# Four moved steps in a one-core hybrid encoder step: DRAM copies of T4, the load of T1, a convolution gate, a reciprocal

## The chip, the cores and the metric

The kernel runs on one core of a Trainium2 chip. The metric is the device time of one execution in microseconds (us). Three executions of the kernel before took 1503.79, 1504.84 and 1506.19 us; the median, 1504.84 us, is the time to compare with. A further execution was taken by the hardware profiler.

The engines have the names of the profile: PE is TensorE (matrix products), PEld its weight load, DVE is VectorE, ACT is ScalarE, POOL is GpSimd, and SP is the queue from which most DMAs are issued. Each engine runs its own instructions in order and waits on semaphores for the others.

## What is computed

One layer of an encoder, for 1024 prompt frames and 32 sample frames (1056 columns in all), in float32:

```python
h = rmsnorm(x, g_mix)
proj = h @ w_in                                   # q, k, v, cb, cc, cx, ga, gc
y_attn = attend(q, k, v).reshape(b, t, SB_WIDTH) @ w_attn_out
conv_out, new_buf = causal_conv(cc * cx, conv_buf, conv_w)
y_conv = (cb * conv_out) @ w_conv_out
merged = jax.nn.sigmoid(ga) * y_attn + jax.nn.sigmoid(gc) * y_conv
x = x + merged @ w_o
f = jnp.square(jax.nn.relu(rmsnorm(x, g_ffn) @ w_up)) @ w_down
x = x + f
x = x + jax.nn.sigmoid(rmsnorm(x, g_ple) @ w_ple_gate) * (p @ w_ple)
```

The model width is 1024, the inner width of the MLP 4096. The outputs are the normed x, the keys, the values and the last convolution inputs.

## The kernel before, in words

**Products.** Activations lie with features on the 128 partitions and frames along the free dimension. Each float32 operand is split into a high and a low part (a copy to fp32r on ScalarE, a subtraction on VectorE), and a product is three matmuls: high by high, high by low, low by high. The large products, `x @ w_in` and the `w_up` half of the MLP, are done by a scheme of Strassen's kind (Winograd's form): of the quarters of weights and activations, sums (S1 to S4, T1 to T4) are formed, and seven products replace eight. Two sets of 256 output features are run together as a pair (`seven_pair`, L560); within a pair part of the products is split once more, by the operands called inner (`prepare_inner`, L256) and last (`prepare_last`, L298, `last_operands`, L336).

**Steps.** `seven_pair` is a generator that yields after each product of 12 matmuls, 25 times in a pair. `run` (L809) takes one step of it and then one step of every generator on the list `side`, in the order of the list. All the other work hangs on this list: loads of the next weights, their splits, what follows a set's outputs (scaling by the inverse norm, gates, stores). `after(n, ...)` (L772) puts a generator off by n steps. Where an instruction stands in the program is therefore a matter of yields. The order on PE, DVE, ACT and POOL is kept as written throughout, that on SP in the stage of the `w_up` pairs 2 to 15 (L2631).

**The buffers.** Most tiles of one row of 1056 columns come from one pool of 37 buffers (`blk`, L93). A new tile takes a buffer that was released before, and its first writer waits until the last reader of the old tile is done, a DMA among them.

**Around T4 and T1 (pairs of the `w_up` stage).** In pair 2 and 3 the operand T4 is used whole. From pair 4 on (`both`, L2003) its product too is split, and needs operands that are built once, during pair 2, 3, by `last_operands("u", ...)` (L2636): it starts one step late, fetches raw T-sums from DRAM (`rlu`, L2636 in the profile), copies blocks of T4 to the DRAM tiles zduB11, zduB21 and zduB22 (L348, six DMAs of 264 KB on SP; there is no B12), and then, twice, forms sums on VectorE (L354, L357), a high part `dlu` on ScalarE (L362), a low part on VectorE (L366), and stores both to the DRAM tile zduT (L368). The first of the two rounds begins its sums at step 7 of the pair, the second at step 14; its stores are issued at step 17. In each later pair, `z_load` (L372) brings these blocks back into SBUF (ztB, ztT; L374): B11 after the first product, T1 after the third, the rest later. `outer("A11", "B11")` uses the first in step 8, `outer("S1", "T1")` the second in step 9 (L634, L645). The copies ACT L635, L647 and L653 free the PSUM tile that the next group needs. Of the previous set, `mid_sums` (L1943) forms three sums and a difference on VectorE and stores them from SP (mdT, L1948 to L1957), `up_hooks` stores the squared outputs (mdB, L1968). The weights of the next pair are loaded into four raw buffers (raw_u4r, raw_u4o, raw_u4e and so on; L115, L212, L207) and split or summed by `prepare` (L217).

**Around the convolution's gate.** `conv_gate` (L1166), for the four column blocks nb of cb, scales (L1079, in `scaled`), multiplies by the convolution's result (L1169), waits 8 steps for odd and 3 for even nb, makes the high part `cvh` (ACT, L1173) and issues its store from ScalarE's queue (L1174), and a step later makes the low part (DVE, L1176) and stores it from SP (L1177). Behind it come the keys of the next set, `keys_or_queries` (L1083), whose scaling is again L1079 and whose high parts are L1089 to L1093.

**Around the reciprocal.** `stats_x` (L956) squares the rows of x on ScalarE, takes the root (ACT, L967) and the reciprocal (DVE, L968) of the nine sums per partition, waits six steps, and spreads the result over the columns.

Of the kernel before, what the change touches and what calls it, by code (L numbers as in the profile page):

```python
# [9 lines left out]
F32 = mybir.dt.float32  # L10
# [65 lines left out]
def tile_step(  # L76
# [8 lines left out]
    nc = tc.nc  # L85
# [7 lines left out]
    def blk(name, dt=F32, shape=None):  # L93
        return bpool.tile(shape or [P, T], dt, tag="B", name=name)
# [56 lines left out]
    quarters = [slice(t * TQ, (t + 1) * TQ) for t in range(4)]  # L151
    oper = {k: [None] * 4 for k in ("B11", "B12", "B21", "B22", "T1", "T2", "T3", "T4")}
# [183 lines left out]
    def last_operands(nm, load):  # L336

        def fetch_raw(k):
            r = blk(f"rl{nm}{k}", F32, [P, 4, TQ])
            for i in range(2):  # L340
                load(r[:, 2 * i : 2 * i + 2, :], k + 2 * i)
            return r

        raw = fetch_raw(0)
        for b, j0, f in (("B11", 0, 0), ("B21", 2, 0), ("B22", 2, 1), ("B12", 0, 1)):
            if b in zd[nm]:
                for j in range(2):
                    nc.sync.dma_start(zd[nm][b][:, :, j, :], oper["T4"][j0 + j][:, :, quarters[f]].bitcast(F32))  # L348
        for k in range(2):
            for _ in range(5 - k):  # L350
                yield
            x = [raw[:, i, :] for i in range(4)]
            for o, a, b, op in ((3, 3, 1, sub), (1, 0, 1, sub)):
                dve(x[o], x[a], x[b], op=op)  # L354
            yield
            for o, a, b, op in ((0, 0, 3, add), (2, 2, 0, sub)):
                dve(x[o], x[a], x[b], op=op)  # L357
            yield
            d, done_ = blk(f"dl{nm}{k}", F32R, [P, 4, TQ]), raw
            if k == 0:  # L360
                raw = fetch_raw(1)
            nc.scalar.copy(d, done_)  # L362
            yield
            for h in range(2):
                c = slice(2 * h, 2 * h + 2)
                dve(done_[:, c, :].bitcast(F32R), done_[:, c, :], d[:, c, :].bitcast(F32), op=sub)  # L366
            for part, src in ((0, d.bitcast(F32)), (1, done_)):
                nc.sync.dma_start(zd[nm]["T"][:, :, part, k, :].rearrange("a p t -> p a t"), src)  # L368

    zt = {}  # L370

    def z_load(nm, b):  # L372
        zt[b] = t = blk(f"zt{b}", F32R, [P, 2, 2, TQ])
        nc.sync.dma_start(t.bitcast(F32), zd[nm]["T"]["T2 T1 T4 T3".split().index(b)] if b[0] == "T" else zd[nm][b])  # L374
# [185 lines left out]
    def seven_pair(s0, s1, key, m, last, after=({}, {}), both=None, more=None):  # L560
# [13 lines left out]
        def inner(a, b, on=None, pool_=few):  # L574
            return inner_product(f"{a}{key}", ws[key][a], b, on, pool_)

        def done(i, k):
            after[i].get(k, int)()
# [14 lines left out]
        def third(i, t):  # L593
            product(i, "S2", "T2", t, x[i][t])
            u2[i][t] = tile_of("u2", t)
            nc.scalar.copy(u2[i][t], x[i][t])  # L596

        def fourth(i, t):
            product(i, "S3", "T3", t, x[i][t])
            dve(m(i, 1)[:, q[t][2]], x[i][t], s5[i][t], op=sub)  # L600

        def fifth(i, t):
            product(i, "S4", "B22", t, z[i][t])
            dve(m(i, 0)[:, q[t][2]], u2[i][t], z[i][t], op=sub)
# [5 lines left out]
        def outer(a, b, on=None, pool_=few):  # L610
            return inner_product(f"l{a}{key}", ws[f"{key}l"][a], zt.pop(b), on, pool_)
# [4 lines left out]
        def seven_both():  # L616
            for f in (first, second):
                for t in range(2):
                    f(0, t)
                    yield  # L620
                    if f is first and t == 0:
                        z_load(both, "B11")
                    if f is second and t == 0:
                        z_load(both, "T1")
            third(0, 0)
            yield
            third(0, 1)
            yield
            fourth(0, 0)
            yield  # L630
            tmp = blk(f"tmp{key}", F32, [P, 4, TQ])
            p4, s4, u4 = (tmp[:, i, :] for i in range(3))
            v4 = wpool[0].tile([P, TQ], F32, tag="v4", name=f"v4{key}", bufs=1)
            xl = outer("A11", "B11", pool_=tps)  # L634
            nc.scalar.copy(p4, xl)  # L635
            fourth(0, 1)
            yield
            z_load(both, "T2")
            z_load(both, "B21")
            done(0, "22")  # L640
            xi = inner("A11", "B11")
            dve(p1[0], xi, p1[0], op=add)
            fifth(0, 0)
            yield
            zl = outer("S1", "T1")  # L645
            z_load(both, "B22")
            nc.scalar.copy(s4, zl)  # L647
            fifth(0, 1)
            done(0, "12")
            yield  # L650
            zi = inner("S1", "T1")
            i5 = tile_of("s5", 2)
            nc.scalar.copy(i5, zi)  # L653
            inner("S2", "T2", xi)
            dve(p1[1], xi, p1[1], op=add)
            yield
            outer("S2", "T2", xl)
            dve(v4, xl, s4, op=sub)
            c11 = inner("A12", "B21", pool_=many)
            dve(m(0, 0)[:, q[0][1]], c11, p1[0], op=add)  # L660
            yield
            c[1] = tile_of("p1", 2)
            inner("S3", "T3", xi)
            dve(c[1], xi, i5, op=sub)
            outer("A12", "B21", x[0][0])
            fold(0, 0, p4)
            yield
            z_load(both, "T3")
            second(1, 0)
            yield  # L670
            inner("S4", "B22", zi)
            dve(m(0, 0)[:, q[1][1]], p1[1], zi, op=sub)
            done(0, "11")
            first(1, 1)
            yield
            c[0] = tile_of("p1", 3)
            inner("A22", "T4", xi)
            nc.scalar.copy(c[0], xi)
            outer("S4", "B22", x[0][1])
            fold(0, 1, v4)  # L680
            yield
            z_load(both, "T4")
            done(0, "21")
            first(1, 0)
            done(1, "11")
            yield
            second(1, 1, few)
            yield
            outer("S3", "T3", xl)
            dve(v4, xl, s4, op=sub)  # L690
            nc.scalar.copy(u4, xl)
            third(1, 1)
            yield
            third(1, 0)
            yield
            fifth(1, 1)
            yield
            fourth(1, 0)
            yield
            fifth(1, 0)  # L700
            done(1, "12")
            done(1, "near")
            yield
            fourth(1, 1)
            outer("A22", "T4", x[1][0])
            fold(1, 1, v4)
            fold(1, 0, u4)
            done(1, "22")
            done(1, "21")
            yield  # L710
            for k in (s0, s1, key, f"{key}l"):
                ws.pop(k)
# [243 lines left out]
    def stats_x():  # L956

        nc.vector.memset(ssq, 1.0)
        for i in range(9):
            n = P if i < 8 else DEC  # L960
            r = rows[i % 3][:n, :]
            nc.scalar.activation(r, r, AF.Square, accum_out=ssq[:n, i : i + 1])
            if i < 6:
                load_rows(i + 3)
            for _ in range(3 if i in (2, 5) else 1):
                yield
        nc.scalar.activation(rst, ssq, AF.Sqrt, bias=eps_t, scale=1.0 / D)  # L967
        nc.vector.reciprocal(rst, rst)  # L968
        for _ in range(6):
            yield  # L970
        nc.scalar.preload_act_table_set("sigmoid_and_others")
        for q0 in (0, 3, 6):
            yield from spread(rst, rs, q0)
            yield
# [8 lines left out]
    def md(k, s_):  # L983
# [11 lines left out]
    zd = {  # L995
        nm: {k: dpool.tile([P, 2, 2, TQ], F32, name=f"zd{nm}{k}") for k in ("B11", "B21", "B22")}
        for nm in ("u",)
    }
# [167 lines left out]
    def conv_gate(nb, m):  # L1166
        scaled(m)
        yield
        dve(m, m, cst.pop(("y", nb)), op=ALU.mult)  # L1169
        for _ in range(8 if nb % 2 else 3):  # L1170
            yield
        h = blk(f"cvh{nb}", F32R)
        nc.scalar.copy(h, m)  # L1173
        nc.scalar.dma_start(cvd[nb, 0], h.bitcast(F32))  # L1174
        yield
        dve(m.bitcast(F32R), m, h.bitcast(F32), op=sub)  # L1176
        nc.sync.dma_start(cvd[nb, 1], m)  # L1177
        yield
# [561 lines left out]
    with tc.manual_schedule(engines=MM):  # L1740
        next(sample)
        for n in range(len(steps) + LAG + 1):
# [13 lines left out]
            for op in ORDER:  # L1756
# [9 lines left out]
                elif op == "G" and n > LAG and steps[n - LAG - 1][2] % 2 == 1:  # L1766
                    p, j, i_ = steps[n - LAG - 1]
# [248 lines left out]
    first = {}  # L2016
# [632 lines left out]
    with tc.manual_schedule(engines=MM):  # L2649
# [68 lines left out]
        for u in range(8, 23):  # L2718
            t = u // 8 - 1
# [84 lines left out]
```

## Time and profile before

| what | value |
|---|---|
| median of three executions | 1504.84 us |
| the profiled execution | 1508.1 us |
| its span, first to last instruction | 1506.2 us |
| mean granted TensorE clock | 0.999 |
| DVE, ACT, POOL busy | 79%, 53%, 25% of the span |
| moved by DMA, mean over the span | 201 GB/s |

The kernel runs through these stages: input products to about 427 us, attention with embedding and convolution products in between to 607 us, branch and output projections to about 747 us, the `w_up` products to about 1070 us, `w_down` to about 1394 us, and the per-layer embedding with the last norm.

How to read it: times of the profile are microseconds from the start of the span, and lines L... are those of the kernel before. A row of the timeline gives start, duration, engine, line and operation, output and inputs by the program's names, the shapes, and in brackets the idle time of the engine just before it and what ended it. That releaser is inferred from semaphores: of several that a wait needs it is the one that came last by the profile. SPq and ACTq are the DMA issues of those queues. Matmuls overlap their predecessors, so a busy TensorE shows rows that start every 0.12 us though each lasts 0.28.

### The profile page before, as it was taken

What the parts mean: (1) busy time and instruction counts of PE and PEld (TensorE: products, weight loads), DVE (VectorE), ACT (ScalarE), POOL (GpSimd) and SP (SyncE); (2) the same over time, 40 slices, a digit from 0 to 9 for tenths busy, and PEclk for the clock granted to TensorE, in tenths of its full rate; (3) what the DMA queues carried; (4) which work ended last, traced back from release to release, by engine and by line L of the source; (5) the groups of instructions that cost most, each with busy time, mean ns of one, the idle gap of its engine ahead of it and who ended that gap; (6) DMA issues with size and microseconds to landing.
All of it is one profiled execution on the core that took longest, in us unless ns stands there. A gap on an engine that the chain in (4) does not pass through costs nothing.

```text
span 1506.2 us, 29625 instructions
## 1 busy us (share of the span) xinstructions
PE 1489.3 (99%) x11520; PEld 1475.5 (98%) x11520; DVE 1187.2 (79%) x1716; ACT 802.8 (53%) x1595; POOL 378.3 (25%) x326
## 2 busy tenths in 40 slices
PE   9999999999999999999999999999999999999997
PEld 8999999999999999999999999999999999999997
DVE  6867689779578999876788777888688878879766
ACT  7654444444467767433475555565655433334655
POOL 0433334445121223003323334334000000000251
PEclk9999999999999999999999999999999999999999
DMA  6624425422688666745647677766979767855433
GB/s 242 209 79 171 157 71 190 155 81 100 216 273 262 188 168 153 264 143 187 231 156 258 238 243 258 250 229 233 374 288 284 241 192 237 293 185 167 141 130 121
DMA packets 127772, 303.37 MB, mean 201 GB/s; under 512 B 14960, under 2 KB 35568, under 8 KB 127632
## 3 DMA queue, kind: packets, MB, share of 16 engines
q1 hardware_dynamic: 122512, 286.97, 56.3%
q0 software_dynamic: 1728, 6.29, 2.4%
q10 hardware_dynamic: 3392, 8.23, 1.7%
q8 instruction: 90, 1.47, 0.4%
q14 instruction: 50, 0.41, 0.1%
HBM read 219.89 MB, written 89.93 MB: 206 GB/s over the span
## 4 chain that ended last, share of the span: by engine, by line
PE 89%; DVE 4%; ACT 3%; DMA 3%; issue 1%; ACTq 0%; SPq 0%; DVEq 0%
PE ps_dn L2232 6%; PE ps_dn L2233 6%; PE ps_dn L2231 6%; PE ps_A11i L453 4%; PE ps_A11i L454 4%; PE ps_A11i L455 4%; PE ps_A11u L453 3%; PE ps_A11u L454 3%; PE ps_A11u L455 3%; PE av L1495 3%; PE ps_wo L133 2%; PE ps_wo L135 2%; PE ps_wo L134 2%; PE ps_S1i L455 2%; PE ps_S1i L454 2%; PE pa L1476 2%
## 5 line engine op out<-in xcount | busy, mean ns | idle before, releaser
L2232 PE MATMUL ps_dn<-flP,whi_dn 128*128 128x264 f32 x768 | 218.3, 284 | 0.0
L2231 PE MATMUL ps_dn<-fhP,whi_dn 128*128 128x264 f32 x768 | 218.3, 284 | 0.0
L2233 PE MATMUL ps_dn<-fhP,wlo_dn 128*128 128x264 f32 x768 | 218.3, 284 | 0.0
L2231 PEld LDWEIGHTS ps_dn<-fhP,whi_dn 128*128 128x128 f32 x768 | 144.5, 188 | 0.0
L2233 PEld LDWEIGHTS ps_dn<-fhP,wlo_dn 128*128 128x128 f32 x768 | 144.5, 188 | 0.0
L2232 PEld LDWEIGHTS ps_dn<-flP,whi_dn 128*128 128x128 f32 x768 | 144.5, 188 | 0.0
L1440 DVE TENSOR_TENSOR_SCAN r<-r 128x128 f32<-128x128 f32 (+3 forms) x64 | 86.9, 1358 | 5.3 <-POOL r L1433 5.3
L2446 POOL TENSOR_TENSOR xx<-xx,pgs 128x400 f32<-128x400 f32 (+1 forms) x17 | 20.0, 1184 | 281.5 <-DVE pgs L2445 281.5
L453 PE MATMUL ps_A11i<-T,shS_i 128*128 128x264 f32 x288 | 82.4, 286 | 0.7 <-ACT u_i L596 0.7
L455 PE MATMUL ps_A11i<-T,slS_i 128*128 128x264 f32 x288 | 82.0, 285 | 0.4 <-DVE slS_i L251 0.4
L454 PE MATMUL ps_A11i<-T,shS_i 128*128 128x264 f32 x288 | 82.2, 285 | 0.0
L453 PE MATMUL ps_A11u<-T,shS_u 128*128 128x264 f32 x256 | 73.1, 286 | 1.8 <-ACT u_u L596 1.7
L454 PE MATMUL ps_A11u<-T,shS_u 128*128 128x264 f32 x256 | 72.9, 285 | 0.0
L455 PE MATMUL ps_A11u<-T,slS_u 128*128 128x264 f32 x256 | 72.7, 284 | 0.0
L2075 ACT CAST whi_dn<-raw_dn 128x1024 fp32r<-128x1024 f32 x31 | 32.6, 1052 | 69.8 <-PE ps_dn L2232 51.1
L1433 POOL TENSOR_SCALAR_AFFINE_SELECT r<-r 128x128 f32<-128x128 f32 x64 | 37.6, 588 | 127.8 <-ACT r L1426 127.8
L2097 DVE TENSOR_TENSOR flP<-mrP,fhP 128x1056 fp32r<-128x1056 f32 x48 | 60.1, 1251 | 2.7 <-ACT fhP L2092 2.6
L135 PE MATMUL ps_wo<-mh,wlo_wo 128*128 128x352 f32 x192 | 62.0, 323 | 0.0
L134 PE MATMUL ps_wo<-ml,whi_wo 128*128 128x352 f32 x192 | 61.9, 323 | 0.0
L133 PE MATMUL ps_wo<-mh,whi_wo 128*128 128x352 f32 x192 | 61.8, 323 | 0.0
L251 DVE TENSOR_TENSOR slS_i<-s_i,shS_i 128x512 fp32r<-128x512 f32 x54 | 48.3, 895 | 13.2 <-ACT shS_i L191 12.8
L1480 DVE TENSOR_TENSOR at<-pa,at 128x512 fp32r<-128x512 f32 (+2 forms) x96 | 50.3, 546 | 10.3 <-ACT at L1479 9.4
(2058 smaller groups left out, 5825.1 us busy)
## 6 DMA issues: line engine op xcount, KB each, us to landing
raw_dn<-in_w_down_dram SPq DMA_DIRECT2D x59, 512.0 KB, 5.4
mrP<-mdT SPq DMA_DIRECT2D x32, 528.0 KB, 5.9
mdB<-m SPq DMA_DIRECT2D x48, 264.0 KB, 2.5
ztT<-zduT SPq DMA_DIRECT2D x24, 528.0 KB, 5.4
mrP<-mdB SPq DMA_DIRECT2D x24, 528.0 KB, 6.2
ztB<-zduB SPq DMA_DIRECT2D x18, 528.0 KB, 4.9
s<-gd SPq DMA_DIRECT2D x16, 528.0 KB, 6.1
mdT<-ta SPq DMA_DIRECT2D x32, 264.0 KB, 2.3
```

What stands on the lines that cost most here:

```text
L133: nc.tensor.matmul(ps, wh, xh[k][:, cols], start=(k == order[0]), stop=False)
L134: nc.tensor.matmul(ps, wh, xl[k][:, cols], start=False, stop=False)
L135: nc.tensor.matmul(ps, wl, xh[k][:, cols], start=False, stop=(k == order[-1]))
L453: nc.tensor.matmul(p_, wh[:, k, :], h, start=new and n == 0, stop=False, **on)
L454: nc.tensor.matmul(p_, wh[:, k, :], l, start=False, stop=False, **on)
L455: nc.tensor.matmul(p_, wl[:, k, :], h, start=False, stop=z, **on)
L1440: nc.vector.tensor_tensor_scan(rev, rev, rev, 1.0, ALU.mult, ALU.bypass)
L1480: nc.vector.tensor_tensor(al, pt[:, :nb, :], ah.bitcast(F32), op=ALU.subtract)
L2097: dve(l, mraw.pop(v), opd[v].bitcast(F32), op=sub)
L2231: nc.tensor.matmul(ps, hi[:, j, :], oh, start=j == 0, stop=False)
L2232: nc.tensor.matmul(ps, hi[:, j, :], ol, start=False, stop=False)
L2233: nc.tensor.matmul(ps, lo[:, j, :], oh, start=False, stop=j == NP_ - 1)
```

## The change

The six copies of T4's blocks move from the start of `last_operands`, behind its first two loads, to its end, behind the second round's stores; there is a yield before each block, and the entry for B12, which had no effect, goes. In `seven_both` the load of T1 is issued after the second product of the pair instead of the third. `stats_x` yields once between the root and the reciprocal, and once less after it. `conv_gate` waits 7 steps instead of 8 for odd blocks.

```diff
@@ last_operands
         raw = fetch_raw(0)
-        for b, j0, f in (("B11", 0, 0), ("B21", 2, 0), ("B22", 2, 1), ("B12", 0, 1)):
-            if b in zd[nm]:
-                for j in range(2):
-                    nc.sync.dma_start(zd[nm][b][:, :, j, :], oper["T4"][j0 + j][:, :, quarters[f]].bitcast(F32))
         for k in range(2):
...
             for part, src in ((0, d.bitcast(F32)), (1, done_)):
                 nc.sync.dma_start(zd[nm]["T"][:, :, part, k, :].rearrange("a p t -> p a t"), src)
+        for b, j0, f in (("B11", 0, 0), ("B21", 2, 0), ("B22", 2, 1)):
+            yield
+            for j in range(2):
+                nc.sync.dma_start(zd[nm][b][:, :, j, :], oper["T4"][j0 + j][:, :, quarters[f]].bitcast(F32))
@@ seven_pair
                     f(0, t)
                     yield
-                    if f is first and t == 0:
-                        z_load(both, "B11")
-                    if f is second and t == 0:
-                        z_load(both, "T1")
+                    if f is first:
+                        z_load(both, "T1" if t else "B11")
@@ stats_x
         nc.scalar.activation(rst, ssq, AF.Sqrt, bias=eps_t, scale=1.0 / D)
+        yield
         nc.vector.reciprocal(rst, rst)
-        for _ in range(6):
+        for _ in range(5):
             yield
@@ conv_gate
-        for _ in range(8 if nb % 2 else 3):
+        for _ in range(7 if nb % 2 else 3):
             yield
```

## The prediction, made before the result

> **What bounds the kernel now.** I read the page first, then the list of waits of TensorE, then its timeline, from which every start that came late can be read with its place.
>
> ```profile
> span 1506.2 us, 29625 instructions
> PE 1489.3 (99%) x11520; PEld 1475.5 (98%) x11520; DVE 1187.2 (79%) x1716; ACT 802.8 (53%) x1595; POOL 378.3 (25%) x326
> ```
>
> TensorE is busy for 99% of the span, and the change neither adds nor removes a matmul. Time can only come from, or go to, the moments at which a matmul starts late. These are the ones inside the stages that the change touches (start, duration; in brackets the idle time before it and its releaser):
>
> ```profile
> 82.75 0.39 PE L455 MATMUL ps_A11i<-T,slS_i 128*128 128x264 f32 x1 [0.38 <-DVE slS_i L251]
> 251.52 0.39 PE L453 MATMUL ps_A11i<-T,shS_i 128*128 128x264 f32 x1 [0.66 <-ACT u_i L596]
> 808.68 0.39 PE L437 MATMUL ps_inA11u2y<-yiT3m,whi_u2y 128*128 128x264 f32 x1 [0.45 <-DVE p_u L733]
> 821.61 0.39 PE L453 MATMUL ps_A11u<-T,shS_u 128*128 128x264 f32 x1 [1.71 <-ACT u_u L596]
> 966.83 0.36 PE L437 MATMUL ps_inlS1u10y<-ztT,lxu10yl 128*128 128x264 f32 x1 [1.34 <-DMA ztT<-zduT]
> 969.68 0.39 PE L437 MATMUL ps_inS1u10y<-yiT1m,whi_u10y 128*128 128x264 f32 x1 [0.44 <-ACT tmpu10y L647]
> ```
>
> Their sum, 0.38 + 0.66 + 0.45 + 1.71 + 1.34 + 0.44 = 4.98 us, is the most that these edits can return. Each edit is worth what it takes off its own late start, and only if nothing else is late next.
>
> **T4's copies (up_pair 2, 3).** The six copies leave the SP queue at step 2 of the pair and come back, two each, at steps 18, 19 and 20 of its 25.
>
> ```profile
> 794.45 4.56 SPq L348 DMA_DIRECT2D zduB<-T  x6
> 799.11 1.14 SPq L1951 DMA_DIRECT2D mdT<-m  x1
> 804.42 0.43 DVE L604 TENSOR_TENSOR m<-u_u,ps_S1u 128x264 f32<-128x264 f32 x1 [1.60 <-DMA mdT<-m]
> 805.85 1.08 ACT L362 CAST dlu<-rlu 128x1056 fp32r<-128x1056 f32 x1 [7.29 <-DVE m L604]
> 808.54 0.68 DVE L251 TENSOR_TENSOR slA_u<-raw_u2e,shA_u 128x512 fp32r<-128x512 f32 x1
> 810.18 1.75 SPq L207 DMA_DIRECT2D raw_u4e<-in_w_up_dram  x2
> 813.72 0.68 DVE L251 TENSOR_TENSOR slS_u<-s_u,shS_u 128x512 fp32r<-128x512 f32 x1
> 816.27 0.69 DVE L253 TENSOR_TENSOR s_u<-raw_u4e,raw_u4r 128x512 f32<-128x512 f32 x1 [1.87 <-DMA raw_u4e<-in_w_up_dram]
> 817.81 1.08 ACT L362 CAST dlu<-rlu 128x1056 fp32r<-128x1056 f32 x1 [3.33 <-DVE rlu L357]
> 821.20 0.36 ACT L596 COPY u_u<-ps_A11u 128x264 f32<-128x264 f32 x1
> ```
>
> Read downwards, this is one chain. The copies hold SP for 4.56 us, so the store of m (L1951) and the stores behind it start at 799 instead of 794. VectorE idles 1.60 us for that store until 804.42. ScalarE idles 7.29 us until 805.85; the L604 named there comes later in the program, so it is another wait, by my reading for a buffer of the full pool that one of these stores still reads. Hence L251 at 808.54 is late, the buffer of raw_u2e comes free late, raw_u4e is issued only at 810.18, and L253 idles 1.87 us for it. Behind L253 stand L357, the second dlu, and the copy at 821.20 for which TensorE waited 1.71 us.
>
> Without the six issues the store can go 799.11 - 794.45 = 4.66 us sooner, which is more than the 1.60 us of idle time. So L251 at 808.54 comes at least 1.60 us sooner, raw_u4e is issued and lands that much sooner, and L253 moves from 816.27 to 814.67 or better. It can't pass L251 in VectorE's order, which ends at 813.72 + 0.68 and follows TensorE, itself 0.45 us ahead by then: at best 813.95. L253 and all behind it thus gain 1.60 to 2.32 us, and the copy ends between 821.56 - 2.32 = 819.24 and 819.96. TensorE would want it at 821.61 - 1.71 - 0.45 = 819.45, so 0 to 0.5 us of that late start remain. L733 at 808.68 is behind the same idle time, and its 0.45 us goes. The edit returns 1.65 to 2.16 us; I take 2.1, nearer the upper end, because more than the 1.60 us is freed on ScalarE.
>
> What the copies meet at the new place:
>
> ```profile
> 821.17 1.81 SPq L1968 DMA_DIRECT2D mdB<-m  x2
> 831.37 0.41 SPq L374 DMA_DIRECT2D ztB<-zduB  x1
> L437 PE MATMUL ps_inlA11u4y<-ztB,lwu4yl x2: 284/284/284, 840.7 to 841.1; 128*128 128x264 f32 x2
> ztB<-zduB SPq DMA_DIRECT2D x3, 528.0 KB, 4.9
> ```
>
> They queue about where L1968 stands, ahead of the load of raw_u5r, four stores of mid_sums and the first ztB load. At worst they push all of it by the whole 4.56 us. The ztB load would then be issued at 831.37 + 4.56 = 835.93 and land 0.41 + 4.9 us later, at 841.2, against 840.7 - 2.16 = 838.5 in TensorE's earlier time: a loss of 2.7 us. At best SP's gaps swallow them: of the 831.37 - 821.17 - 1.81 = 8.4 us in between, six other issues of at most 0.41 us leave 5.9 us free, against 4.56 us of copies. I take no loss, because the gap is the larger; both ends are kept. The pool's order of release does not change: T4 is still read by the pair's last two steps.
>
> **T1's load, a step sooner, in six pairs.** It passes what the side generators issue in that step.
>
> ```profile
> 960.05 0.38 SPq L1951 DMA_DIRECT2D mdT<-m  x1
> 960.52 0.41 SPq L374 DMA_DIRECT2D ztT<-zduT  x1
> 962.64 0.32 SPq L1957 DMA_DIRECT2D mdT<-tb  x1
> 968.22 0.62 ACT L305 CAST lyu10yl<-raw_u10r 128x512 fp32r<-128x512 f32 x1 [4.35 <-DMA ztB<-zduB]
> 969.26 0.37 ACT L647 COPY tmpu10y<-ps_inlS1u10y 128x264 f32<-128x264 f32 x1
> ```
>
> In pair 10, the only one in which TensorE waits for it, the load passes one store: 960.52 - 960.05 = 0.47 us of SP, plus its share of the data ahead. That takes 0.47 to 1.34 us off the late start at 966.83. But the next matmul group waits for L647 at 969.26, which stands in ScalarE's order behind L305 at 968.22. L305 does not read ztB; it takes a buffer of the full pool, by the order of release that of tb, whose store was issued at 962.64 and is not moved. A TensorE that starts 1.34 us sooner at 966.83 waits 0.44 + 1.34 us at 969.68. Between 0 and 1.78 us, I take 0.1: what is returned at the first wait is paid at the second.
>
> **Convolution's gate.** For odd blocks cvh, its store and the subtraction L1176 move one step ahead.
>
> ```profile
> 242.95 1.07 ACT L1173 CAST cvh<-m_i 128x1056 fp32r<-128x1056 f32 x1
> 243.08 1.82 DVE L251 TENSOR_TENSOR slS_i<-s_i,shS_i 128x512 fp32r<-128x512 f32 x1
> 244.83 2.35 DVE L1176 TENSOR_TENSOR m_i<-m_i,cvh 128x1056 fp32r<-128x1056 f32 x1
> 246.13 2.19 POOL L253 TENSOR_TENSOR s_i<-raw_i12r,raw_i11e 128x512 f32<-128x512 f32 x1
> 247.09 2.34 DVE L1079 TENSOR_TENSOR m_i<-m_i,rs 128x1056 f32<-128x1056 f32 x1
> 249.47 0.62 ACT L1089 CAST kh<-m_i 128x512 fp32r<-128x512 f32 x1 [2.06 <-DVE m_i L1079]
> ```
>
> TensorE's 0.66 us at 251.52 hangs on L596, behind L1089, behind L1079, behind L1176. VectorE and GpSimd take turns here: L1079 starts at 247.09 but ends at 249.43, about 1.1 us after GpSimd's operation ended at 248.32. Moved ahead, L1176 runs before L251, and one turn of GpSimd fewer falls ahead of L1079: 1.14 us, from L1176's end at 247.18 to 248.32. Against this, what stood before cvh on ScalarE now comes at most its 1.07 us and its issue later, and with it the subtraction L251 at 243.08; its product is two steps off, which covers that, and without that cover TensorE would lose up to 1.07 us. So the edit lies between a loss of 0.4 us and a return of 0.66 us; I take 0.66, as 1.14 us is well over it. The second gate pair, near 367, has no late start to remove.
>
> **Reciprocal.**
>
> ```profile
> 80.71 1.37 POOL L253 TENSOR_TENSOR raw_i4r<-raw_i4r 128x512 f32<-128x512 f32 x1
> 81.94 0.21 DVE L968 RECIPROCAL rst<-rst 128x9 f32<-128x9 f32 x1 [1.02 <-ACT rst L967]
> 82.07 0.63 DVE L251 TENSOR_TENSOR slS_i<-s_i,shS_i 128x512 fp32r<-128x512 f32 x1
> ```
>
> The 1.02 us of idle time ahead of L968 goes, but GpSimd's operation runs until 82.08, just when L251 starts now. If L251 has to wait for it, as L1079 did, it ends at 82.08 + 0.6 = 82.68 instead of 82.70. Ends 0 and 0.38 us; I take 0.05, by the row of L1079. L968 itself, 0.21 us, moves behind work that is there anyway, and what reads its result is not moved: the six yields in all remain. The Trainium skill, "SBUF — State Buffer", section "SBUF: two separate sides", has the pair of ports shared by VectorE and GpSimd as an exclusive lock that the first holds for its whole instruction; the durations above agree, and by it this edit returns nothing.
>
> **The sum.** 2.1 + 0.1 + 0.66 + 0.05 = 2.9 us. The profiled execution would fall from 1508.1 to 1505.2 us, its span from 1506.2 to 1503.3; it lies 3.26 us above the median of the runs, 1504.84, which I move by the same 2.9 to 1501.9 us. A measurement of this kernel tells 0.2%, 3.0 us, from no change: the forecast lies just inside it.
>
> **Rivals.** *All late starts go.* Pair 10's tb store lands sooner once T1 is off the rings, L305 with it, and L251 at 82.07 does not wait: 1504.84 - 4.98 = 1499.9 us. For it speaks that the wait of L305 ends with a ztB load that was issued behind the tb store; against it, that no byte ahead of that store goes.
>
> *The copies are late at their new place.* The 2.7 us above are paid, and 0.2 us are returned: 1504.6. Half of that loss gives 1503.3. In the same place lands the case that the edit does not do what it says, because the rings and not SP's issues held the stores back.
>
> *Slower: T1 ahead of the stores.* In pairs 8 and 12 L647 ends just before TensorE needs it:
>
> ```profile
> 927.52 0.37 ACT L647 COPY tmpu8y<-ps_inlS1u8y 128x264 f32<-128x264 f32 x1
> 928.09 0.28 PE L437 MATMUL ps_inS1u8y<-yiT1m,whi_u8y 128*128 128x264 f32 x1
> 1008.77 0.37 ACT L647 COPY tmpu12y<-ps_inlS1u12y 128x264 f32<-128x264 f32 x1
> 1009.27 0.31 PE L437 MATMUL ps_inS1u12y<-yiT1m,whi_u12y 128*128 128x264 f32 x1
> ```
>
> The slack is 0.2 us in pair 8 and 0.1 in pair 12. If T1's 528 KB ahead of the stores make each pair's tb store late by a fraction of the load's own 4.9 us (ztB's, the same size), say half, these two and pair 10 pay 2.45 us less 0.15 of slack each: 6.9 - 2.9 = 4.0 us slower, 1508.8. It decides from 1.1 us a pair, and by more than 0.2% from 2.1 us. Against it: tb's store is issued 2 us and more behind T1 in pair 10. The Trainium skill, "DMA: Bandwidth & Descriptors", section "Queues, rings and completion order", has a DMA's semaphore land only after every earlier write of that engine, which speaks for this rival; no row here separates the two.
>
> **How the numbers follow.** The forecast, 2.2 to 3.6 us returned, 0.50, about its middle of 2.9; all late starts go, 0.17; copies late or without effect, 0.27; slower, 0.06. Over 3.0 us are returned in a little under half of the first case and in all of the second: 0.23 + 0.17 = 0.40. Slower by over 3.0 us is most of the last: 0.05. The rest is 0.55. The range goes from 1500.2, just short of the second case's end, to 1504.6, the third's; outside lie the slower rival, the full 4.98 us and an edit without any effect.
>
> **What would show it.** Right: no late start near 808 and 820, raw_u4e issued before 808.6; none near 251, with L1079 ending near 248.2; a late start of about 1.8 us, in one or two pieces, still at pair 10; L251 still ending near 82.7. Wrong: a late start at the first inlA11u4, at pair 4's stores, or at inS1 of pairs 8, 12 and 14.

## The result and the profile after

The changed kernel takes 1502.66 us, median of 22 runs (1500.84 to 1506.40), and the kernel before 1504.68 us, median of 22 (1503.37 to 1506.19). The ratio is 0.9987, with a 95% interval from 0.9982 to 0.9993: 2.0 us faster, between 1.1 and 2.7 us. The interval leaves out 1, but the gain is less than the 0.2%, 3.0 us, that the prediction asks of a change, so by that measure it counts as no change. The profiled execution took 1503.25 us against 1508.1.

The head of the page, after:

```profile
span 1501.5 us, 29617 instructions
PE 1488.6 (99%) x11520; PEld 1475.6 (98%) x11520; DVE 1188.5 (79%) x1716; ACT 803.9 (54%) x1595; POOL 381.9 (25%) x326
```

The late starts with a bracket that TensorE still has in the stages of the change (timeline of TensorE, after; lines of unchanged code are up to 4 lower than in the kernel before; the timeline prints no bracket for the shortest waits):

```profile
961.41 0.36 PE L437 MATMUL ps_inlS1u10y<-ztT,lxu10yl 128*128 128x264 f32 x1 [0.73 <-DMA ztT<-zduT]
964.69 0.39 PE L437 MATMUL ps_inS1u10y<-yiT1m,whi_u10y 128*128 128x264 f32 x1 [0.86 <-ACT tmpu10y L645]
1063.14 0.39 PE L453 MATMUL ps_A11u<-T,shS_u 128*128 128x264 f32 x1 [0.39 <-ACT u_u L596]
```

Of the six of before, those at 82, 251, 808 and 821 are gone, pair 10's two are there with 1.59 us in all instead of 1.78, and one at 1063 is new. The chain around T4, from the timelines of VectorE, ScalarE and SP, after:

```profile
792.48 0.40 SPq L1950 DMA_DIRECT2D mdT<-m  x1
800.48 1.08 ACT L358 CAST dlu<-rlu 128x1056 fp32r<-128x1056 f32 x1 [3.95 <-DVE rlu L353]
800.71 0.42 DVE L604 TENSOR_TENSOR m<-u_u,ps_S1u 128x264 f32<-128x264 f32 x1
803.57 0.68 DVE L251 TENSOR_TENSOR slA_u<-raw_u2e,shA_u 128x512 fp32r<-128x512 f32 x1
804.66 1.83 SPq L207 DMA_DIRECT2D raw_u4e<-in_w_up_dram  x2
811.58 0.68 DVE L253 TENSOR_TENSOR s_u<-raw_u4e,raw_u4r 128x512 f32<-128x512 f32 x1
816.49 0.37 ACT L596 COPY u_u<-ps_A11u 128x264 f32<-128x264 f32 x1
816.98 1.69 SPq L368 DMA_DIRECT2D zduB<-T  x2
819.46 1.50 SPq L368 DMA_DIRECT2D zduB<-T  x2
821.76 1.40 SPq L368 DMA_DIRECT2D zduB<-T  x2
827.06 0.62 SPq L374 DMA_DIRECT2D ztB<-zduB  x1
```

L604 and L253 no longer wait (1.60 and 1.87 us before), ScalarE waits 3.95 instead of 7.29 us and then for VectorE, raw_u4e is issued at 804.66, and the copies stand between the stores further down.

So far the forecast seems to hold step by step. But the profiled executions differ by 4.9 us and the medians by 2.0: one execution of each does not give the size of an effect. The experiments look for what makes the difference.

### The profile page after: what moved, and what is told of

The parts are those of the page before. It is cut to its first block, busy times and chain, and to the rows that moved or that the text cites. A ratio compares the mean times of both kernels' runs of the same rounds, so it can differ in the third digit from the quotient of the medians.

```text
span 1501.5 us, 29617 instructions
## 1 busy us (share of the span) xinstructions
PE 1488.6 (99%) x11520; PEld 1475.6 (98%) x11520; DVE 1188.5 (79%) x1716; ACT 803.9 (54%) x1595; POOL 381.9 (25%) x326
## 4 chain that ended last, share of the span: by engine, by line
PE 93%; DVE 3%; ACT 2%; DMA 1%; issue 1%; ACTq 0%; DVEq 0%; SPq 0%
PE ps_dn L2232 6%; PE ps_dn L2230 6%; PE ps_dn L2231 6%; PE ps_A11i L454 5%; PE ps_A11i L453 5%; PE ps_A11i L455 5%; PE ps_A11u L453 3%; PE ps_A11u L454 3%; PE ps_A11u L455 3%; PE av L1494 2%; PE ps_S1i L454 2%; PE ps_S1i L455 2%; PE ps_S1i L453 2%; PE ps_wo L133 2%; PE ps_wo L135 2%; PE ps_wo L134 2%
## 5 line engine op out<-in xcount | busy, mean ns | idle before, releaser
L2074 ACT CAST whi_dn<-raw_dn 128x1024 fp32r<-128x1024 f32 x31 | 32.6, 1051 | 68.4 <-PE ps_dn L2231 51.2
L251 DVE TENSOR_TENSOR slS_i<-s_i,shS_i 128x512 fp32r<-128x512 f32 x54 | 51.1, 947 | 12.3 <-ACT shS_i L191 12.0
```

Of the source, the lines that this page charges most:

```text
L251: lows.pop()()
```

## Experiments

Each run has a profile of its own, so that with the two above there are fourteen executions. My theory after the result is "B" in the expectations: the late starts are partly chance, and the profiled execution of before had nearly all of them at their worst. The rival, "A", is that they belong to the program and return in every execution.

### The kernel before once more

> The kernel before, unchanged, profiled a second time. Theory A (the late starts are of the program, the same in every execution): those at 251, 808, 821 and pair 10 come again with 0.66, 0.45, 1.71 and 1.34 + 0.44 us, each within 0.2; the one at 82.75 hangs on the load of xr, which landed 0.91 us late there, and need not. Theory B (the profiled execution, 3.4 us above the median, had more of them than an ordinary one): the sum of these late starts is at least 1 us smaller than 4.98. Timed, it is the same kernel: ratio 1.000, and its interval shows what five rounds can tell.

Ratio 0.9998 (0.9989 to 1.0007). The median of these eleven runs is 1503.49 us, and that of the other 33 runs of the same kernel in these rounds 1504.53: medians of this size differ by 1 us without any change. The span of this execution is 1501.1 us instead of 1506.2. In the stages of the change TensorE has one late start with a bracket left; its rows with their neighbours:

```profile
817.50 0.28 PE L455 MATMUL ps_A11u<-T,slS_u 128*128 128x264 f32 x1
819.09 0.39 PE L453 MATMUL ps_A11u<-T,shS_u 128*128 128x264 f32 x1 [1.31 <-ACT u_u L596]
819.32 0.28 PE L454 MATMUL ps_A11u<-T,shS_u 128*128 128x264 f32 x1
819.44 0.29 PE L455 MATMUL ps_A11u<-T,slS_u 128*128 128x264 f32 x1
```

Theory A falls. The rows also show the price of a late start: matmuls start every 0.12 us, but here two steps took 1.59 and 0.23 us, 1.58 us more than 0.24, where the bracket says 1.31. The bracket counts from the modelled end of the matmul before, 0.28 us after its start, and the step behind the pause is longer too: 0.27 us come on top of each bracket.

### Each part alone

The four parts of the diff, one at a time, on the kernel before. T4's copies:

```diff
@@ last_operands: the copies behind the second round's stores
-        for b, j0, f in (("B11", 0, 0), ("B21", 2, 0), ("B22", 2, 1), ("B12", 0, 1)):
...
+        for b, j0, f in (("B11", 0, 0), ("B21", 2, 0), ("B22", 2, 1)):
+            yield
...
```

> The kernel before with only T4's copies moved. Theory A: the late starts near 808 and 821 are gone, and with each goes 0.27 us more than its bracket, the time in which TensorE comes back to one matmul per 0.12 us: 0.72 + 1.98 = 2.7 us, median near 1502.0; 251 keeps its 0.66 and pair 10 its 1.8. Theory B: the same places in the trace, but 1.0 to 1.7 us in the median, 1503.0 to 1503.7. Rival (copies late at their new place): a late start at the first inlA11u4 or at pair 4's stores, and under 1 us returned.

The gate:

```diff
-        for _ in range(8 if nb % 2 else 3):
+        for _ in range(7 if nb % 2 else 3):
```

> The kernel before with only the convolution's gate a step sooner. Both theories: L1079 ends near 248.2, no late start near 251, while 808, 821 and pair 10 keep theirs. Theory A: 0.66 + 0.27 = 0.9 us in the median, 1503.8. Theory B: 0 to 0.9 us. Rival (cvh on ScalarE delays the sums ahead of it): a new late start between 240 and 252 or near 367 and under 0.3 us returned.

T1's load:

```diff
-                    if f is first and t == 0:
-                        z_load(both, "B11")
-                    if f is second and t == 0:
-                        z_load(both, "T1")
+                    if f is first:
+                        z_load(both, "T1" if t else "B11")
```

> The kernel before with only T1's load sooner. My theory (returned at the first wait, paid at the second): in pair 10 the late start at inlS1 falls from 1.34 to about 0.7 us, that at inS1 rises from 0.44 to about 0.9, 0.2 us is returned, and lyu10yl still waits for the store of tb. Median 1504.5. Rival (T1 ahead of the stores): late starts at inS1 of pairs 8, 12 or 14 and a median above 1505. Other rival (the edit returns all of it): both late starts below 0.3 us, median 1503.2.

The reciprocal:

```diff
+        yield
         nc.vector.reciprocal(rst, rst)
-        for _ in range(6):
+        for _ in range(5):
```

> The kernel before with only the reciprocal a unit later. If the edit takes the late start at 82 away, there is none even where ScalarE's two waits for xr add up to more than 0.9 us. If the late start hangs on xr's load alone, it is there when the sum is above 0.9 us (about the sum less 0.87) and absent below, with the edit as without it. In both cases L251 there starts at once and ends with GpSimd's operation plus about 0.6 us, as it did in the changed kernel, and the median is within 0.5 us of 1504.5.

Ratios: T4's copies 0.9994 (0.9985 to 1.0003), gate 0.9994 (0.9985 to 1.0003), T1's load 1.0002 (0.9994 to 1.0011), reciprocal 0.9996 (0.9987 to 1.0004). None is told from 1 by itself; the sum of the four, -0.0014, fits the -0.0013 of the change, though each of them is uncertain by 0.0009.

Against the expectations: T4's copies came out at Theory B's end (1503.70 us), with no late start at 808, 821 or pair 4. With the gate alone none is left near 251, and none is new there or near 367; that at 821 stays with 1.44 us, but at 808 there is no bracket. With T1's load alone my theory missed: pair 10 has no bracket, where 0.7 and 0.9 us were expected. That is the trace of the rival by which all of it is returned, but not its median (1504.04 us instead of 1503.2); the slower rival did not come. With the reciprocal alone the waits for xr added up to 0.21 us, so the case that would tell its two readings apart did not arise, and its median, 1503.85, lies 0.65 us from 1504.5 instead of within 0.5.

### The changed kernel twice more, and without T1's move

> The changed kernel, unchanged, profiled a second time. Theory B (which late starts an execution has, and how large, is partly chance: it hangs on when loads and stores land): none at 251, 808 and 821 again, since the edits took their causes away; the one at 82 comes if the two waits of ScalarE for xr add up to more than about 0.9 us, as in all five executions so far, and stays away below; pair 10 may show anything between 0 and 1.6 us. Theory A (the same in every execution): 0.73 and 0.86 at pair 10 and 0.39 at 1063 come again within 0.2.

> The changed kernel a third time. If T1's move delays the store of tb, that store lands later after its issue in pair 10 than without the move (4.8 and 5.5 us against 3.1 to 4.4 so far), and inS1 of pair 10 starts 0.5 us late or more. If that was chance, the late start is anything between 0 and 1.1 us. Median 1502.0 to 1503.0.

The edit of the next two, on the changed kernel:

```diff
-                    if f is first:
-                        z_load(both, "T1" if t else "B11")
+                    if f is first and t == 0:
+                        z_load(both, "B11")
+                    if f is second and t == 0:
+                        z_load(both, "T1")
```

> The changed kernel with T1's load back in its old place. If T1's move is worth nothing, the ratio is that of the change itself, 0.9987, within the uncertainty, and pair 10 shows anything between 0 and 1.8 us, with T1's load issued behind the store of m. If the move costs something by delaying the stores, the ratio is below 0.998 and the stores of pairs 8 to 14 land sooner.

> The same kernel as e7_no_t1 (T4's copies, gate and reciprocal, T1 in its old place) once more, beside a third timing of the changed kernel, because 1501.3 against 1503.0 us lay within the spread. If T1's move costs something, this one is 0.3 to 1 us faster than the changed kernel again, and pair 10's late start at inS1 stays at or below 0.45 us. If T1's move costs nothing, the two medians lie within 0.3 us.

Ratios: changed kernel 0.9981 (0.9973 to 0.9990) and 0.9981 (0.9971 to 0.9992), medians 1502.96 and 1502.66 us; without T1's move 0.9981 (0.9972 to 0.9990) and 0.9986 (0.9977 to 0.9995), medians 1501.34 and 1502.28 us. In none of these four executions is there a bracket at 251, 808 or 821; the second without T1's move has a start at 818 that is late by the 0.27 us alone. Pair 10's brackets add up to 1.12 and 0.43 us with the move; without it there is one of 0.32 us, and none in the second execution. Pair 10 thus changes from one execution to the next, as Theory B has it, and the third changed execution (0.43 us) is the case of chance.

### T1's load two units sooner

```diff
-                    if f is first:
-                        z_load(both, "T1" if t else "B11")
+                    if f is first and t == 0:
+                        z_load(both, "B11")
+                        z_load(both, "T1")
```

> The changed kernel with T1's load another unit sooner, right behind the load of B11. If what delays the store of tb is the 528 KB of T1's load that are still on their way when the store is issued, this load is off the queues sooner, no late start is left at inlS1, and that at inS1 of pair 10 falls below 0.5 us: 0.3 to 0.8 us faster than the changed kernel. If every load ahead of the stores costs the same, or more because two loads now stand together, the store of m and the copy behind it come later still: late starts at inS1 of several pairs, and 0.5 to 3 us slower than the changed kernel.

Ratio 0.9988 (0.9979 to 0.9997), median 1502.43 us; pair 10 has no late start. That is the first case's trace, but not its gain of 0.3 to 0.8 us: the median is 0.2 us below that of the changed kernel in the same rounds (1502.66), and the ratio the higher of the two.

### The twelve executions side by side

Stages are measured from the start of the first matmul of one named group to that of another, so that only what TensorE lost in between changes them: first ps_g to first ps_inS1i3y ("14 to 92"), on to ps_inA11i11y ("92 to 254") and to ps_inS1i17y ("254 to 381"); first ps_inA11u2y to first ps_inA11u4y ("799 to 843": in the profile of before 842.94 - 799.32 = 43.62), and on to ps_inS1u12y ("843 to 1009"). The second column is the sum of ScalarE's waits for xr (the brackets of L962). The two runs of the next sections are left out. All in us.

| execution | xr | 14 to 92 | 92 to 254 | 254 to 381 | 799 to 843 | 843 to 1009 |
|---|---|---|---|---|---|---|
| before | 1.26 | 78.57 | 161.57 | 126.64 | 43.62 | 166.33 |
| before, second | 0.76 | 78.14 | 160.74 | 126.65 | 42.77 | 163.98 |
| T4 only | 1.14 | 78.49 | 161.44 | 126.64 | 40.95 | 164.02 |
| gate only | 0.60 | 77.99 | 160.65 | 126.39 | 43.06 | 164.96 |
| T1 only | 1.45 | 78.77 | 161.38 | 126.65 | 42.00 | 164.42 |
| reciprocal only | 0.21 | 77.80 | 161.22 | 126.64 | 41.94 | 164.22 |
| changed | 0.54 | 77.78 | 160.65 | 126.40 | 40.96 | 165.96 |
| changed, second | 1.03 | 78.35 | 160.65 | 126.39 | 40.97 | 165.26 |
| changed, third | none | 77.82 | 160.65 | 126.39 | 40.97 | 164.80 |
| without T1's move | 0.39 | 77.82 | 160.65 | 126.40 | 40.96 | 164.60 |
| the same, second | 0.50 | 77.83 | 160.62 | 126.39 | 41.22 | 164.87 |
| T1 two units sooner | 1.05 | 78.36 | 160.62 | 126.39 | 40.96 | 163.92 |

Read down the columns. *T4* (799 to 843): with the copies in their old place 41.94 to 43.62, mean 42.68; moved, 40.95 to 41.22, mean 41.00. The edit returns 1.7 us on average, from 0.9 to 2.6 by the execution (the 41.22 holds the late start at 818). *Gate* (92 to 254): 160.74 to 161.57, mean 161.27, against 160.62 to 160.65, and from 254 to 381 another 126.64 - 126.39 = 0.25 in every execution: 0.9 us in all. *Reciprocal* (14 to 92): with and without the edit the stage goes by xr alone, 77.8 as long as the waits stay at 0.54 or less, then from 77.99 at 0.60 to 78.77 at 1.45, about 0.9 us for each us; 1.03 and 1.05 with the edit (78.35, 78.36) lie within 0.05 us of the line through 0.76 and 1.14 without it (78.14, 78.49). In these two the start at 82 is late too, without a bracket. The edit returns 0.05 us at most. *T1* (843 to 1009): 164.42 to 165.96, mean 165.1, with the move; 163.98 to 166.33, mean 164.7, without.

### The cast of ly a step later

```diff
@@ prepare_last
         yield
         yield
+        yield
         low = pair_of(ra, "ly", ("S2", "S4"))
         yield
         low()
-        for _ in range(8):
+        for _ in range(7):
             yield
```

> The changed kernel with the cast of ly a step later in prepare_last, so that ScalarE's copy of the outer S1 product (L645) stands ahead of it. If it is the order on ScalarE that lets the second wait of pair 10 take up what the first returns, no late start at inS1 of pair 10 is left, whatever the store of tb does: at best 0.86 + 0.27 = 1.1 us off the worst executions, 0.5 us in the median (ratio 0.998). If the cast is then late itself, a late start appears at the outer S2 product of pairs 4 to 14, L439 on lyu, and the ratio is that of the change or worse.

Ratio 1.0024 (1.0016 to 1.0033), median 1508.73 us. The late start at inS1 of pair 10 is gone, and each of the pairs 4 to 14 has one of 0.86 to 0.88 us at the outer S2 product. Pair 10, ScalarE, VectorE and TensorE, lines 1 higher than in the changed kernel:

```profile
964.61 0.38 ACT L646 COPY tmpu10y<-ps_inlS1u10y 128x264 f32<-128x264 f32 x1 [0.58 <-PE ps_inlS1u10y L440]
964.89 0.62 ACT L305 CAST lyu10yl<-raw_u10r 128x512 fp32r<-128x512 f32 x1
967.89 0.68 DVE L330 TENSOR_TENSOR lyu10yl<-raw_u10r,lyu10yl 128x512 fp32r<-128x512 f32 x1
968.63 0.39 PE L440 MATMUL ps_inlA11u10y<-ztT,lyu10yl 128*128 128x264 f32 x1 [0.88 <-DVE lyu10yl L330]
```

Both halves of the expectation came: the order on ScalarE is what ties inS1 to the store of tb, and ly a step later is late for its own product. Six pairs at 0.88 + 0.27 us make 6.9 us; pair 10's own late start goes off again, and 6.1 us separate the medians of this and the changed kernel.

### T4's copies twice at the new place

```diff
             yield
-            for j in range(2):
+            for j in (0, 1, 0, 1):
```

> The changed kernel with each of T4's copies written twice at the new place: 12 issues instead of 6 in pair 2, 3. The prediction counted 5.9 us of free time of SP there against 4.56 us of copies. If that count holds, the second six, 4.56 us more, push the load of B11 back by 2 to 4.6 us past the free time, and the first inlA11 of pair 4 starts 0.5 to 3 us late. If the queue there has more room than counted, no late start appears at pair 4 and the time is that of the changed kernel, 1502.6.

Ratio 1.0055 (1.0039 to 1.0070), median 1512.44 us. It is late, but one step sooner than expected and for another reason:

```profile
817.27 5.73 SPq L368 DMA_DIRECT2D zduB<-T  x4
828.67 1.59 SPq L368 DMA_DIRECT2D zduB<-T  x2
834.23 1.28 SPq L368 DMA_DIRECT2D zduB<-T  x2
837.64 0.62 ACT L305 CAST lwu4yl<-raw_u4r 128x512 fp32r<-128x512 f32 x1 [6.60 <-DMA zduB<-T]
839.91 0.59 PE L453 MATMUL ps_A11u<-T,shS_u 128*128 128x264 f32 x1 [4.87 <-ACT u_u L596]
843.41 0.59 PE L437 MATMUL ps_inlA11u4y<-ztB,lwu4yl 128*128 128x264 f32 x1 [0.49 <-DMA ztB<-zduB]
```

ScalarE waits 6.60 us for the copies, because lwu4yl takes the pool buffer of T4's last block, which the last copy reads. It goes on 2.1 us after SP has issued this one (834.23 + 1.28 = 835.51). In the changed kernel the last copy is issued at 822.49 and lands 6.0 us later, at 828.5; the cast starts at 830.65 without a wait. This cover of about 2 us is what the edit lives on, and not SP's free time ahead of the load of B11. The load of B11 is late as well, but costs only 0.49 us.

The doubled copies do more than take twice the issues: each second pair writes the same blocks as the pair before it and waits for it to land. Between 828.67 + 1.59 = 830.26 and 834.23 SP issues nothing, and the first copy of the pair before lands at 834.22. So the run shows who waits when the copies are late, but does not test the count of 5.9 us of free time.

## Why the prediction was right, and where not

**The sum.** Forecast 2.9 us, measured 2.0 (1.1 to 2.7). The terms by the table: T4 1.7 instead of 2.1, gate 0.9 instead of 0.66, reciprocal 0 to 0.05 as forecast, T1 nothing to -0.4 instead of 0.1. The 2.0 us lie just below the 2.2 to 3.6 of the forecast's own case and above what the late copies would have left, in a gap between the two. What failed is a step that all terms share: the median of the runs, "which I move by the same 2.9". The profiled execution lay 3.4 us above the median of before (1508.1 against 1504.68), and I moved the median by what that execution alone had lost; its stage from 799 to 843 is the longest of five. The missing 0.27 us of each late start worked the other way: with it, 4.98 us was not "the most that these edits can return", nor did that sum hold the starts whose bracket is empty. The two errors have opposite signs, so it is luck that the sum came out this near.

**T4.** The chain was right from the stores to L596: with the six issues gone, VectorE's two waits in it go, and of the late starts at 808 and 821 nothing is left in six of seven executions and 0.27 us in one, where I had kept 0 to 0.5 us. What no run separates is whether SP's 4.56 us of issues held the stores back or the copies' data did: the move took both away. That the new place costs nothing was right, but "the pool's order of release does not change" was wrong: after, TensorE's last matmul on T4 ends at 825.9 and the last copy lands at 828.5, so the copies become the last readers of T4's buffers. That it is covered, by about 2 us, is luck: the prediction did not look there.

**Gate.** Right in mechanism: after, L1078 has one turn of GpSimd fewer ahead of it and ends at 244.93 + 2.35 = 247.28, which with the 0.86 us by which this execution was ahead is 248.1, against the forecast 248.2:

```profile
242.06 1.25 DVE L1175 TENSOR_TENSOR m_i<-m_i,cvh 128x1056 fp32r<-128x1056 f32 x1
243.23 1.78 DVE L251 TENSOR_TENSOR slS_i<-s_i,shS_i 128x512 fp32r<-128x512 f32 x1
244.54 1.62 POOL L253 TENSOR_TENSOR raw_i12r<-raw_i12r 128x512 f32<-128x512 f32 x1
244.93 2.35 DVE L1078 TENSOR_TENSOR m_i<-m_i,rs 128x1056 f32<-128x1056 f32 x1
```

But in the second execution of before the old order also ended at 247.38, because there L251 and GpSimd's operation started together and VectorE did not have to wait first. In the first execution GpSimd's operation started 0.02 us ahead of L251, and L251 took 1.82 us instead of 0.69. The first row is of that one, the others are of the second:

```profile
243.06 1.29 POOL L253 TENSOR_TENSOR s_i<-raw_i11e,raw_i12r 128x512 f32<-128x512 f32 x1 [1.57 <-DVE wlo_i11y L290]
242.16 0.69 DVE L251 TENSOR_TENSOR slS_i<-s_i,shS_i 128x512 fp32r<-128x512 f32 x1
242.16 1.83 POOL L253 TENSOR_TENSOR s_i<-raw_i11e,raw_i12r 128x512 f32<-128x512 f32 x1 [1.57 <-DVE wlo_i11y L290]
245.03 2.35 DVE L1079 TENSOR_TENSOR m_i<-m_i,rs 128x1056 f32<-128x1056 f32 x1
```

So the first gate returns 0.1 to 0.9 us. And "the second gate pair, near 367, has no late start to remove" was wrong. It has one whose bracket is empty (kernel before):

```profile
374.21 0.28 PE L455 MATMUL ps_A11i<-T,slS_i 128*128 128x264 f32 x1
374.50 0.39 PE L453 MATMUL ps_A11i<-T,shS_i 128*128 128x264 f32 x1
374.72 0.28 PE L454 MATMUL ps_A11i<-T,shS_i 128*128 128x264 f32 x1
```

Two steps of 0.29 and 0.22 us instead of 0.12 each are 0.27 us lost, the 0.25 of the table.

**Reciprocal.** Right, though the trace of after looks otherwise. The late start at 82 is gone there, but because xr landed sooner, as the table shows. L251 did what was forecast: it starts while GpSimd works and ends 0.55 us after it (79.84 + 1.36 = 81.20 and 79.97 + 1.78 = 81.75).

```profile
79.84 1.36 POOL L253 TENSOR_TENSOR raw_i4r<-raw_i4r 128x512 f32<-128x512 f32 x1
79.97 1.78 DVE L251 TENSOR_TENSOR slS_i<-s_i,shS_i 128x512 fp32r<-128x512 f32 x1
83.46 0.20 DVE L967 RECIPROCAL rst<-rst 128x9 f32<-128x9 f32 x1
```

The rule of the Trainium skill, "SBUF — State Buffer", section "SBUF: two separate sides", that the first of the two engines holds the shared ports for its whole instruction, agrees with these rows.

**T1.** The two profiled executions look as forecast: 1.34 + 0.44 became 0.73 + 0.86, returned at the first wait and paid at the second, because ScalarE's cast of ly stands ahead of L645 and waits for tb's store:

```profile
957.74 0.32 SPq L1956 DMA_DIRECT2D mdT<-tb  x1
963.22 0.62 ACT L305 CAST lyu10yl<-raw_u10r 128x512 fp32r<-128x512 f32 x1 [1.01 <-DMA mdT<-tb]
```

That order is shown by the run with the cast later. That the sizes agree is chance: the kernel before has no bracket at pair 10 in its second execution, and T1 only has none either.

The rival that T1 ahead of the stores delays one of them was right, but for the store of m and not that of tb: T1's load now stands just ahead of it. ScalarE's copy of the outer A11 product (L635, after L633) then waits for this store. In pair 6, the first row of the kernel before, the others after:

```profile
881.75 0.38 ACT L635 COPY tmpu6y<-ps_inlA11u6y 128x264 f32<-128x264 f32 x1 [1.87 <-PE ps_inlA11u6y L439]
872.42 0.44 SPq L374 DMA_DIRECT2D ztT<-zduT  x1
872.95 0.51 SPq L1950 DMA_DIRECT2D mdT<-m  x1
877.87 0.38 ACT L633 COPY tmpu6y<-ps_inlA11u6y 128x264 f32<-128x264 f32 x1 [2.56 <-DMA mdT<-m]
```

In T1 only and the three executions of the changed kernel the copy waits for the store in five of the six pairs each: 1.61 to 2.93 us outside pair 10, and 3.48 to 5.28 us in it. Without the move, and with the load two units sooner, it does so in pair 10 alone, 1.16 to 2.07 us. TensorE hardly feels it: there is no bracket at inS1 of pairs 8, 12 and 14. What it costs in pair 10 stays open. All runs together, the changed kernel has a median of 1502.66 us (44 runs) and the version without the move 1502.16 us (22 runs), but where the two ran side by side, their ratios are equal once and in the other order once (0.9981 and 0.9981, 0.9981 and 0.9986). If it is anything, it is about 0.5 us.

**The rivals.** That all late starts go came about in no execution of the changed kernel: pair 10 had 1.59, 1.12 and 0.43 us. That the copies are late at the new place did not happen either, and the run with the copies doubled shows from where it would. That moving them has no effect is ruled out by the stage from 799 to 843, which is shorter in every execution with the move than in any without.

**The start at 1063** is not of one part of the change: T4 only, T1 only and reciprocal only have it too, with 0.34, 0.32 and 0.24 us. It follows the wait of ScalarE's first w_down block for raw_dn (L2074, L2075 before): 3.43 us of wait go with 0.22 us at TensorE (changed, third) and 3.59 with 0.39 (changed), while the 3.29 us of before leave no bracket. So it hangs on when that load lands.

**Open.** Why loads land sooner in one execution than in another isn't settled: no run changed it. The late starts at 82, 1063 and pair 10 hang on it.

## What to carry to other kernels

Before a late start is priced from one profile, take a second profile of the same kernel: here five of the six late starts of the first had no bracket in the second. Measure a part of a change by the distance between two named matmuls of TensorE around it, over several executions, since a total that varies by 3 us hides parts of 1 us which such a stage can show to 0.03 us (the gate's, with the edit). When a DMA's source is a pool tile, moving the DMA can move the tile's release; look up who takes that buffer next.

## What the hardware showed beyond that

A short stop costs TensorE 0.27 us more than the idle time in the bracket, down to a bracket of nothing (rows at 819 and 374). The Trainium skill, "TensorE: Matmul & The Clock Gate", sections "Single matmul latency" and "Back-to-back issue gap", gives formulas for the latency of a single bf16 matmul and for its isolated gap to the next, and says that in a stream the spacing differs; for 264 columns they make an estimate of 0.276 and 0.113 us. The rows here have 0.28 and 0.12, the first of which is the profile's modelled duration and no measurement. The difference of the rows' own figures, 0.16 us, is the part of the price that the bracket hides; the other 0.11 us is the longer step behind the pause.

A stop of 4.87 us cost about as much again: with T4's copies written twice, the granted clock behind it was 0.50 for 9 us (windows of that run: us, busy of PE, PEld, DVE, ACT and POOL, then the clock, the DMA share and GB/s).

```profile
830.00:835.00 5.00, 5.00 (x42) 4.81 (x40) 0.71 (x1) 0.51 (x2) 1.40 (x2) 1.00 0.59 199
835.00:840.00 5.00, 0.13 (x2) 0.09 (x1) 1.71 (x3) 2.36 (x6) 2.41 (x2) 0.87 0.95 346
840.00:842.00 2.00, 2.00 (x9) 2.00 (x10) 2.00 (x5) 0.75 (x2) 0.38 (x1) 0.50 1.05 228
846.00:848.00 2.00, 2.00 (x11) 2.00 (x11) 0.23 (x1) 0.38 (x1) 0.00 (x0) 0.50 1.06 413
848.00:850.00 2.00, 2.00 (x15) 2.00 (x15) 0.64 (x2) 1.14 (x2) 0.00 (x0) 0.77 0.90 328
```

Matmuls started every 0.22 us there instead of every 0.12. With the 4.87 and 0.49 us of waiting, these 9 us at half the clock, some 4 us lost, explain the 9.8 us between the two medians. The stop of 1.71 us in the kernel before left the clock at 1.00. The same page of the Trainium skill, section "What's actually happening", has the clock halve after at least one idle window of about 3.4 us; this run agrees, for its mean of 0.87 from 835 to 840 puts the halving some 3.7 us into the stop. That page of the Trainium skill has the clock come back after at least one busy window of the same length; here that took 9 us from the first matmul on, with a further wait of 0.49 us in between, so this run does not bear out one window for the way back.
